# A two-layer diffusion backbone: the gating layer's mixing as plain fp32 matmuls, and another issue order

## The chip, the cores and the metric

The kernel runs on one core of a Trainium2 chip. Everything is fp32 in and fp32 out. The metric is the device time of one launch in microseconds; the time of a kernel is the median of several executions. The engines of the core are TensorE (PE, with its weight loads listed as PEld), VectorE (DVE), ScalarE (ACT), GpSimd (POOL) and SyncE (SP, which here only issues DMAs). Each engine works off its own queue in order; engines wait for each other by semaphores.

## The reference

512 latent tokens and 256 context tokens of width 1024 go through two layers. Only the latent tokens of the end are returned.

```python
for i in range(2):
    h = modulate(rmsnorm(x, g0), shift, scale)            # shift, scale, gate: rows of silu(c) @ ada_w[i] + ada_b[i]
    y = window_sink_mixer(h, h_ctx, ...) if i == 0 else chunk_gmlp(h, ...)
    x = x + gate * rmsnorm(y, g1)
    f = swiglu(modulate(rmsnorm(x, g2), shift_f, scale_f), w_in, w_out)     # hidden width 2816
    x = x + gate_f * rmsnorm(f, g3)

def chunk_gmlp(h, w_in, b_in, ln_g, ln_b, w_s, b_s, w_o):
    u, v = split(gelu(h @ w_in + b_in))                   # 512 x 1024 each
    v = layernorm(v, ln_g, ln_b)                          # as 4 chunks of 128 tokens, 8 groups of 128 columns
    mixed = einsum('gpq,bnqgc->bnpgc', w_s, v) + b_s      # per group and chunk: 128x128 by 128x128
    return (u * mixed) @ w_o
```

Layer 0 is attention over windows of 128 tokens and all of the context, with 16 heads on 4 key/value heads and a sink logit for each head. Layer 1 is the gating layer, `chunk_gmlp`, whose mixing the change is about.

## The kernel before, in words

**Precision by splits.** A matmul of the type fp32r takes fp32 operands that have been rounded to fewer bits. Nearly every product in the kernel is made of three of them: each operand is split into a high part (a cast on ACT, `high`, line 217) and the rest (a subtraction on DVE, `low`, line 220), and PE adds high by high, high by low and low by high into one PSUM bank (`mm3`, lines 269 to 271; `mm_a`, line 277). The weights come from HBM in units of 1 MB (`wfetch_N` on the SP queue) into one of two raw buffers, are split in halves (`whigh_N_h` on ACT, `wlow_N_h` on DVE) and are used from the split buffers. The in-projection of the feed-forward network (line 1445) and its out-projection (lines 1623 and 1650) combine blocks of operands first, so that fewer products are needed.

**The order of the work.** The string `ORDER` at line 41 is a list of step names written out by hand. A function hands a step to `at()`, with a rough time; `run_plan()` issues the steps of each stage in the order of the string. As each engine's queue is in order, the string sets what each engine does when, the DMAs of SP and POOL among it. The last projection of a layer (`down`) lies outside of it and is put in order by the framework. A name that comes again in a later stage has `#2` or `#3` behind it.

**The front.** Tiles of x are fetched (`x_fetch_t`, 4 and 5 are the context), normalised (`norm_in_t_z`, line 477 on DVE), turned by PE (`turn_in`, line 500) and modulated; `kv_k_t` are the key and value products of row block k and tile t, `ada0_rows` the first modulation rows.

**The seam between attention and its feed-forward network.** For each of four token tiles t, `ctshift_x_z` makes the modulated input in two halves (DVE, line 1166), `ctturn_z` turns it on PE into a PSUM bank (line 1173), `ctturned_hi` and `ctturned_lo` split it, and `f0head_h_s` are the first in-projection matmuls.

**The gating layer** (lines 1796 to 1947). `v_part` and `u_part` are the two halves of the in-projection; `u_part(u, z)` (lines 1867 to 1874) is 24 matmuls of 512 columns into a PSUM bank. Each of the four `VChain`s (line 1826) takes 128 tokens of v: `add`, `gelu`, `mean`, `var`, `rstd`, `gain` (layer norm times its gain, in place) and `bias` (line 1856, in place); `hi` and `lo` then split the result into `v_hi` and `v_lo`. `ws_in` fetches the mixing weights (512 KB) into one of the two raw buffers of the weight stream, `ws_high` and `ws_low` split them into `ws_hi` and `ws_lo`. `mixed(g)` (line 1883) makes, for group g, four products of 128x128 by 128x128 in one bank, each by `mm3`. `mixed_bias(g)` and `mixed_u(g)` (DVE) add the bias and multiply by gelu(u). The output projection y follows (line 277, weight units 51 to 54).

**The modulation rows** of this layer (`m2`, `m4`) are worked out meanwhile: `fetch_chunk` (SP, 512 KB each, eight of them), `add_chunk` (DVE, line 379), `fold` (a POOL DMA that adds the upper 64 partitions to the lower, line 393), `mirror` (an SP DMA back), `stack` (an ACT cast and a DVE subtraction of 64 partitions), `total` (a matmul with ones into a PSUM bank, line 406) and `done` (DVE or ACT reads the bank, lines 417 and 419).

**PSUM.** The matmul banks come from one pool of eight slots, given out in turn: a step that needs a slot waits until the readers of the bank that had it are done.

Of the kernel before, what the change touches and what calls it, by code (L numbers as in the profile page):

```python
# [14 lines left out]
P = 128  # L15
D = 1024
# [25 lines left out]
x_fetch_4 square_in_4 x_fetch_1 square_in_1 warm_0 rstd_in_4 warm_1 dma rstd_in_1 x_fetch_5 square_in_5 warm_2 warm_3  # L42
rstd_in_5 wfetch_0_0 norm_in_5_1 x_fetch_2 norm_in_4_0 dma#2 norm_in_1_0 turn_in_4_0 square_in_2 norm_in_1_1 warm_4
x_fetch_0 x_fetch_3 square_in_0 norm_in_5_0 turn_in_1_0 rstd_in_2 turn_in_1_1 norm_in_2_0 turn_in_5_0 ada0_fetch_0
turned_in_4_0 square_in_3 rstd_in_0 turned_in_5_0 turned_in_1_0 turn_in_5_1 ada0_rows_0 turn_in_2_0 rstd_in_3
norm_in_2_1 ada0_rows_out_0 norm_in_3_1 <lambda> norm_in_0_0 norm_in_3_0 ada0_cols_0 turn_in_3_1 turned_in_5_1
ada0_fetch_1 turn_in_0_0 norm_in_0_1 ada0_done_0 turn_in_2_1 ada0_fetch_2 whigh_0_0 wfetch_0_1 ada0_rows_1
modulate0_ctx_0 turn_in_0_1 turn_in_3_0 turned_in_3_1 modulated_ctx_0 ada0_rows_out_1 ada0_fetch_3 turned_in_1_1
wlow_0_0 turned_in_2_0 ada0_fetch_4 ada0_cols_1 turned_in_0_0 turned_in_3_0 ada0_rows_2 modulate0_0 wfetch_1 dma#5
# [2013 lines left out]
```

## Time and profile before

| | before |
|---|---|
| time, median of 3 runs | 1115.71 us (1113.52 to 1122.0) |
| the profiled execution: its time | 1122.28 us |
| its span | 1120.5 us |
| its mean granted TensorE clock | 0.993 |
| busy: PE, PEld | 98%, 86% of the span |
| busy: DVE, ACT, POOL | 85%, 55%, 22% |
| HBM | 171.71 MB read, 155 GB/s |

The page of the profile is one execution. Starts in its timelines are microseconds from the start of the span. An engine's row has the start, the duration, the line of the kernel, the operation, output and inputs, the tile sizes, and in brackets the idle time before it with what ended it. Matmuls overlap each other: the time that one costs PE is the distance from its start to the next one's, not its duration. "PEclk" is the clock that TensorE was granted, in tenths of full speed, in 40 slices of 28 us.

### The profile page before, as it was taken

To read this page: it belongs to the slowest core of one execution; us is meant where nothing else is said; L and a number is where in the kernel's file an instruction comes from. 1 tells how busy PE (TensorE), PEld (TensorE's weight loads), DVE (VectorE), ACT (ScalarE), POOL (GpSimd) and SP (SyncE) were. 2 spreads that over 40 slices of the span, in tenths; PEclk is the share of its full clock that TensorE was granted. 3 is DMA by queue.
4 is the path that set the end of the run, shared out by engine and by line. 5 is a ranking of instruction groups with operands and counts; after the bars stand their busy time and mean duration, and the time that the engine had idled before them with its cause. 6 is when DMAs were issued, how large, how long until landed. Compare 5 with 4: busy or idle time off the path is not lost.

```text
span 1120.5 us, 17907 instructions
## 1 busy us (share of the span) xinstructions
PE 1095.7 (98%) x7004; PEld 964.8 (86%) x7004; DVE 957.2 (85%) x1422; ACT 618.5 (55%) x1064; POOL 247.9 (22%) x239
## 2 busy tenths in 40 slices
PE   7999999999999999999999999999999999999997
PEld 4688887777899999997888787888899999998886
DVE  5888989958999999978987778777988898878985
ACT  6357677756555555545655544337555455556652
POOL 1416575624500000001322310005500000002400
PEclk9999999999999999999999999799999999999999
DMA  9642433243345655459954286653134333369821
GB/s 366 255 145 97 162 94 113 76 142 103 114 148 174 206 184 175 161 176 335 223 83 151 101 293 215 180 169 106 47 132 152 132 125 125 147 208 314 174 37 75
DMA packets 49017, 179.69 MB, mean 160 GB/s; under 512 B 4890, under 2 KB 9242, under 8 KB 37796
## 3 DMA queue, kind: packets, MB, share of 16 engines
q1 hardware_dynamic: 41300, 163.60, 42.0%
q0 software_dynamic: 7632, 14.95, 7.7%
q8 instruction: 55, 0.90, 0.3%
q14 instruction: 30, 0.25, 0.1%
HBM read 171.71 MB, written 2.10 MB: 155 GB/s over the span
## 4 chain that ended last, share of the span: by engine, by line
PE 84%; DVE 7%; DMA 3%; ACT 2%; issue 2%; POOL 1%; SPq 0%; DVEq 0%; POOLq 0%; ACTq 0%
PE f L1445 33%; PE y L1623 13%; PE y L277 4%; PE y L1650 4%; PE v L277 4%; PE s_ps L901 3%; PE o_ps L954 3%; PE pT_ps L934 3%; PE q_ps L269 1%; PE q_ps L271 1%; PE q_ps L270 1%; DMA acc<-acc 1%; DVE w_lo L220 1%; PE fa L271 1%; PE fa L269 1%
## 5 line engine op out<-in xcount | busy, mean ns | idle before, releaser
L1445 PE MATMUL f<-H,w_hi 128*128 128x256 f32 x960 | 178.4, 284 | 0.2 <-DVE fc L1456 0.2
L1445 PEld LDWEIGHTS f<-H,w_hi 128*128 128x128 f32 x960 | 149.9, 192 | 1.1 <-DVE fc L1456 0.7
L1445 PE MATMUL f<-H,w_lo 128*128 128x256 f32 x480 | 135.8, 283 | 0.0
L1623 PE MATMUL y<-w_hi,s 128*128 128x512 f32 x448 | 120.1, 389 | 0.0
L1445 PE MATMUL f<-S,w_hi 128*128 128x256 f32 x640 | 118.6, 283 | 0.0
L217 ACT CAST w_hi<-w_raw 128x1024 fp32r<-128x1024 f32 x90 | 94.5, 1052 | 37.7 <-PE v L277 9.7
L217 ACT CAST w_hi<-T 128x1024 fp32r<-128x1024 f32 x80 | 83.6, 1047 | 54.2 <-PE f L1445 32.1
L220 DVE TENSOR_TENSOR w_lo<-w_raw,w_hi 128x1024 fp32r<-128x1024 f32 (+1 forms) x81 | 95.1, 1180 | 8.7 <-ACT w_hi L217 8.7
L1452 ACT COPY fc<-f 128x256 f32<-128x256 f32 x120 | 44.7, 373 | 102.4 <-PE f L1445 99.5
L1445 PEld LDWEIGHTS f<-S,w_hi 128*128 128x128 f32 x640 | 100.0, 192 | 0.1
L1623 PEld LDWEIGHTS y<-w_hi,s 128*128 128x128 f32 x448 | 84.1, 188 | 17.5
L220 DVE TENSOR_TENSOR w_lo<-T,w_hi 128x1024 fp32r<-128x1024 f32 x80 | 97.3, 1216 | 0.0
L1445 PEld LDWEIGHTS f<-H,w_lo 128*128 128x128 f32 x480 | 92.1, 192 | 0.0
L393 POOL DMA_DIRECT2D acc<-acc x9 | 7.8, 862 | 377.2 <-DVE acc L379 371.7
L1445 PE MATMUL f<-S,w_lo 128*128 128x256 f32 x320 | 90.6, 283 | 0.5 <-DVE w_lo L220 0.5
L379 DVE SCALAR_TENSOR_TENSOR acc<-ada_k,sc,acc 128x1024 f32<-128x1024 f32 x56 | 71.6, 1278 | 11.9 <-DMA ada_k<-in_ada 9.8
L1611 POOL DMA_DIRECT2D t<-in_w x48 | 42.3, 938 | 125.3 <-issue 43.2
L1623 PE MATMUL y<-w_lo,s 128*128 128x512 f32 x224 | 69.1, 390 | 0.6 <-DVE w_lo L220 0.6
L1445 PE MATMUL f<-H,x 128*128 128x256 f32 x480 | 64.3, 283 | 0.0
L928 POOL TENSOR_SCALAR p<-p,st 128x512 f32<-128x512 f32 (+1 forms) x64 | 53.3, 850 | 45.6 <-DVE st L924 15.5
L277 PE MATMUL y<-w_hi,st 128*128 128x512 f32 x224 | 62.1, 391 | 0.0
L1445 PEld LDWEIGHTS f<-S,w_lo 128*128 128x128 f32 x320 | 61.4, 192 | 0.7 <-DVE w_lo L220 0.7
(263 smaller groups left out, 2909.7 us busy)
## 6 DMA issues: line engine op xcount, KB each, us to landing
w_raw<-in_w SPq DMA_DIRECT2D x67, 1024.0 KB, 5.1
ada_k<-in_ada SPq DMA_DIRECT2D x56, 512.0 KB, 5.4
ada_raw<-in_ada SPq DMA_DIRECT2D x12, 1024.0 KB, 4.9
w<-in_w SPq DMA_DIRECT2D x12, 1024.0 KB, 9.6
t<-in_w POOLq DMA_DIRECT2D x48, 256.0 KB, 5.7
ada<-in_ada SPq DMA_DIRECT2D x8, 1024.0 KB, 8.0
t<-in_w SPq DMA_DIRECT2D x8, 1024.0 KB, 9.4
w_raw<-in_w SPq DMA_DIRECT2D x10, 512.0 KB, 4.7
```

Of the source, the lines that this page charges most:

```text
L217: nc.scalar.copy(out=hi, in_=src)
L220: (eng or nc.vector).tensor_tensor(out=lo, in0=src, in1=hi.bitcast(F32), op=ALU.subtract)
L277: nc.tensor.matmul(dst, l, w[:, n * 512:(n + 1) * 512], start=first and i == 0, stop=last and i == 2)
L379: nc.vector.scalar_tensor_tensor(out=self.acc, in0=self.raws.pop(k), scalar=sc[:, k:k + 1], in1=self.acc, op0=ALU.mult, op1=ALU.add)
L901: nc.tensor.matmul(dst, self.qT[:, j, :], keys, start=i == 0, stop=i == 1)
L928: nc.gpsimd.tensor_scalar(out=p, in0=p, scalar1=self.st[:, 12 + j:13 + j], scalar2=1.0, op0=ALU.mult, op1=ALU.mult)
L934: nc.tensor.transpose(ps[:, j * P:(j + 1) * P], self.probs[j][:, i * P:(i + 1) * P], ident)
L1445: nc.tensor.matmul(dst, l[:, w], r[:, k, :], start=first and k == 0 and j == 0, stop=k == 3 and j == 2, skip_group_check=True)
L1452: nc.scalar.copy(out=self.c[n][:, i * 256:(i + 1) * 256], in_=self.ps[n, 1 if i == 1 else 0])
L1611: nc.gpsimd.dma_start(out=self.tt[:, p * D + 512 * i:p * D + 512 * (i + 1)], in_=a["w"][F2[self.layer] + 1 + 2 * p + i][:, c:c + 512], acc ...
L1623: nc.tensor.matmul(self.bank7(i, j), st[:, c:c + P], w[:, z * 512:(z + 1) * 512], start=i == 1 and p == 0 and l == 0 and z == 0, stop=p == ...
L1650: nc.tensor.matmul(self.y[t][n], st[:, x + t * P:x + (t + 1) * P], parts[h][w][:, n * 512:(n + 1) * 512], start=v == 0 and h == 0 and i == ...
```

## The change

*Mixing.* The mixing weights are fetched straight into an fp32 tile of their own, `ws`; `ws_high` and `ws_low` go. `VChain.bias` writes its result into one fp32 tile `v`; `hi` and `lo` go for all four tiles. `mixed(g)` calls `nc.tensor.matmul` once for each product, with fp32 operands.

*Order.* In front, the fetches of the two context tiles change places, `kv_0_4` comes earlier, `ada0_fetch_6` and `ada0_rows_3` later; a few first query products and splits swap. In attention and between the layers, some neighbouring steps change places. At the first seam `c1turn_1` moves behind `f0head_0_0`. In the gating layer `ws_in` moves from ahead of m2's third add to just ahead of `u_part_0_1`, and `wfetch_49` comes ahead of `m2fetch_gain`; `m4fetch_0` and `m4start` come behind `m2mirror`; `v2add` comes ahead of `m2done_0`; `m2done_512` moves from there to behind `v3norm`; `wlow_50_0` and `mixed_6` come ahead of the first `mixed_bias`; `whigh_51_0` comes behind `m4stack`, and `u_part_3_1` ahead of `wlow_51_0`.

```diff
@@ ORDER, front
-x_fetch_4 square_in_4 x_fetch_1 square_in_1 warm_0 rstd_in_4 warm_1 dma rstd_in_1 x_fetch_5 square_in_5 warm_2 warm_3
-rstd_in_5 wfetch_0_0 norm_in_5_1 x_fetch_2 norm_in_4_0 dma#2 norm_in_1_0 turn_in_4_0 square_in_2 norm_in_1_1 warm_4
+x_fetch_5 x_fetch_4 square_in_4 x_fetch_1 square_in_1 warm_0 rstd_in_4 warm_1 dma dma#2 square_in_5 warm_2 warm_3
+rstd_in_5 wfetch_0_0 rstd_in_1 x_fetch_2 norm_in_4_0 norm_in_5_1 norm_in_1_0 turn_in_4_0 square_in_2 norm_in_1_1
...
-wlow_0_0 turned_in_2_0 ada0_fetch_4 ada0_cols_1 turned_in_0_0 turned_in_3_0 ada0_rows_2 modulate0_0 wfetch_1 dma#5
-modulated_high_0 turned_in_2_1 ada0_rows_out_2 modulated_low_0 ada0_cols_2 kv_0_2 dma#4 kv_0_3 ada0_done_1
-ada0_fetch_6 kv_0_4 ada0_rows_3 modulated_high_1 modulate0_ctx_1 kv_0_5 ada0_done_2 modulate0_1 modulated_ctx_1
-whigh_0_1 modulated_low_1 norm_in_4_1 turn_in_4_1 m2start ada0_rows_out_3 turned_in_4_1 modulate0_ctx_2 kv_1_2 kv_1_4
...
+wfetch_1 dma#5 kv_0_4 modulated_high_0 turned_in_2_1 ada0_rows_out_2 modulated_low_0 ada0_cols_2 kv_0_2 dma#4 kv_0_3
+ada0_done_1 modulated_high_1 modulate0_ctx_1 kv_0_5 ada0_done_2 modulate0_1 modulated_ctx_1 whigh_0_1 modulated_low_1
+ada0_fetch_6 ada0_rows_3 norm_in_4_1 turn_in_4_1 m2start ada0_rows_out_3 turned_in_4_1 modulate0_ctx_2 kv_1_2 kv_1_4
...
@@ ORDER, first seam
-c2square_x c1turn_0 c3merge c2rstd_x c1turned_hi_0 c1turn_1 c1turned_lo_0 f0first_half_1 f0head_0_0 wfetch_12
+c2square_x c1turn_0 c3merge c2rstd_x c1turned_hi_0 c1turned_lo_0 f0first_half_1 f0head_0_0 c1turn_1 wfetch_12
...
@@ ORDER, gating layer
-wlow_47_0 m2add_chunk_1 v_part_3_(2,) v_part_1_(2,) v0add m2add_chunk_2 v0gelu m2fetch_chunk_5 wlow_47_1 v0mean ws_in
+wlow_47_0 m2add_chunk_1 v_part_3_(2,) v_part_1_(2,) v0add m2add_chunk_2 v0gelu m2fetch_chunk_5 wlow_47_1 v0mean
...
-m2fetch_gain#2 v_part_3_(3,) wlow_48_0 m4fetch_chunk_0 m4start#2 v1var v_part_2_(3,) ws_high m2mirror#2 v1rstd
-wfetch_49 v1gain v0hi ws_low v1norm m2stack#2 m4fetch_chunk_1 v1bias v0lo u_part_0_1 m2total_0_slot m2total_512_slot
-m2done_0#2 m2done_512#2 v2add m4add_chunk_0 m4fetch_chunk_2 whigh_49_0 u_part_1_0 v2gelu v1hi v1lo u_part_1_1 v2mean
+wfetch_49 v1gain m2fetch_gain#2 v_part_3_(3,) wlow_48_0 v1var v_part_2_(3,) m2mirror#2 m4fetch_chunk_0 m4start#2
+v1rstd v1norm m4fetch_chunk_1 v1bias m2stack#2 ws_in u_part_0_1 m2total_0_slot m2total_512_slot v2add m2done_0#2
+m4add_chunk_0 m4fetch_chunk_2 whigh_49_0 u_part_1_0 v2gelu u_part_1_1 v2mean v3add v2var wfetch_50 whigh_49_1
...
-gelu_u_1_1 v2hi v3bias v2lo m4add_chunk_6 v3hi v3lo m4add_chunk_7 m4fold#2 m4fetch_gain#2 mixed_0 whigh_50_1
-mixed_bias_0 mixed_1 mixed_u_0 mixed_bias_1 wlow_50_0 mixed_6 m4mirror#2 mixed_5 mixed_3 mixed_u_1 mixed_4
-mixed_bias_3 gelu_u_2_0 mixed_2 wlow_50_1 whigh_51_0 mixed_u_3 m4stack#2 u_part_3_0 whigh_51_1 mixed_bias_2 mixed_u_2
-wlow_51_0 m4total_0_slot mixed_bias_4 mixed_u_4 mixed_bias_5 gelu_u_2_1 wlow_51_1 mixed_u_5 u_part_3_1 mixed_bias_6
+v3bias m4add_chunk_6 m4add_chunk_7 m4fold#2 m4fetch_gain#2 mixed_0 wlow_50_0 mixed_6 m4mirror#2 whigh_50_1
+mixed_bias_0 mixed_1 mixed_u_0 mixed_bias_1 mixed_5 mixed_3 mixed_u_1 mixed_4 mixed_bias_3 gelu_u_2_0 mixed_2
+wlow_50_1 mixed_u_3 m4stack#2 whigh_51_0 u_part_3_0 whigh_51_1 mixed_bias_2 mixed_u_2 m4total_0_slot mixed_bias_4
+u_part_3_1 wlow_51_0 mixed_u_4 mixed_bias_5 gelu_u_2_1 wlow_51_1 mixed_u_5 mixed_bias_6 m4total_512_slot m4done_0#2
...
@@ gating layer
-    wsh = gp.tile([P, D], F32R, name="ws_hi")
-    wsl = gp.tile([P, D], F32R, name="ws_lo")
-    vhi = gp.tile([P, NT, D], F32R, name="v_hi")
-    vlo = gp.tile([P, NT, D], F32R, name="v_lo")
+    wsp = gp.tile([P, D], F32, name="ws")
+    vn = gp.tile([P, NT, D], F32, name="v")
...
     def ws_in():
-        got["ws"] = raw("ws_raw")[:, 0:D]
-        dma(got["ws"], a["ws"])
-
-    def ws_high():
-        high(wsh, got["ws"])
-
-    def ws_low():
-        low(wsl, wsh, got["ws"])
+        dma(wsp, a["ws"])
...
         def bias(self):
-            nc.vector.scalar_tensor_tensor(out=self.v, in0=self.v, scalar=self.r, in1=rows[2],
+            nc.vector.scalar_tensor_tensor(out=vn[:, self.t, :], in0=self.v, scalar=self.r, in1=rows[2],
                                            op0=ALU.mult, op1=ALU.add)
-
-        def hi(self):
-            high(vhi[:, self.t, :], self.v)
-
-        def lo(self):
-            low(vlo[:, self.t, :], vhi[:, self.t, :], self.v)
...
         for n in range(NT):
-            mm3(ps[:, n * P:(n + 1) * P], vhi[:, n, c], vlo[:, n, c], wsh[:, c], wsl[:, c], True, True)
+            nc.tensor.matmul(ps[:, n * P:(n + 1) * P], vn[:, n, c], wsp[:, c], start=True, stop=True)
```

More of the change, by code (lines that the diff above doesn't have):

```diff
@@ L172 @@
 m2add_chunk_3 v0var v_part_1_(3,) v0gain whigh_48_0 m2add_chunk_4 m2fetch_chunk_6 v0norm m2add_chunk_5 m2fetch_chunk_7
-v_part_2_(2,) v0rstd whigh_48_1 v1add m2add_chunk_6 u_part_0_0 v1gelu m2add_chunk_7 v0bias v1mean m2fold#2 wlow_48_1
-m2fetch_gain#2 v_part_3_(3,) wlow_48_0 m4fetch_chunk_0 m4start#2 v1var v_part_2_(3,) ws_high m2mirror#2 v1rstd
-wfetch_49 v1gain v0hi ws_low v1norm m2stack#2 m4fetch_chunk_1 v1bias v0lo u_part_0_1 m2total_0_slot m2total_512_slot
-m2done_0#2 m2done_512#2 v2add m4add_chunk_0 m4fetch_chunk_2 whigh_49_0 u_part_1_0 v2gelu v1hi v1lo u_part_1_1 v2mean
@@ L197 @@
-f1diff_2_4 c3turned_lo_1#3 f1part_high_2_3 f1head_2_2 f1sum_high_S4 f1part_low_2_1 f1head_3_0 f1sum_low_S4
-f1part_low_2_2 f1head_3_1 f1sum_high_S3 wfetch_58 f1sum_high_S1 f1head_3_2 f1sum_low_S1 f1sum_low_S2 f1part_low_2_3
-f1sum_low_S3
+v_part_2_(2,) v0rstd whigh_48_1 m2add_chunk_6 v1add u_part_0_0 v1gelu m2add_chunk_7 v0bias v1mean m2fold#2 wlow_48_1
+wfetch_49 v1gain m2fetch_gain#2 v_part_3_(3,) wlow_48_0 v1var v_part_2_(3,) m2mirror#2 m4fetch_chunk_0 m4start#2
+v1rstd v1norm m4fetch_chunk_1 v1bias m2stack#2 ws_in u_part_0_1 m2total_0_slot m2total_512_slot v2add m2done_0#2
@@ new lines @@
+m4add_chunk_0 m4fetch_chunk_2 whigh_49_0 u_part_1_0 v2gelu u_part_1_1 v2mean v3add v2var wfetch_50 whigh_49_1
+gelu_u_0_0 v3gelu gelu_u_0_1 v2gain m4add_chunk_1 m4fetch_chunk_3 m4fetch_chunk_4 wlow_49_1 v2rstd m4add_chunk_2
+v3mean wlow_49_0 u_part_2_0 v2norm v3var v2bias m4fetch_chunk_5 wfetch_51 v3rstd m4add_chunk_3 m4add_chunk_4
+m4fetch_chunk_6 u_part_2_1 v3norm m2done_512#2 whigh_50_0 v3gain m4add_chunk_5 m4fetch_chunk_7 gelu_u_1_0 gelu_u_1_1
+v3bias m4add_chunk_6 m4add_chunk_7 m4fold#2 m4fetch_gain#2 mixed_0 wlow_50_0 mixed_6 m4mirror#2 whigh_50_1
@@ new lines @@
+mixed_bias_0 mixed_1 mixed_u_0 mixed_bias_1 mixed_5 mixed_3 mixed_u_1 mixed_4 mixed_bias_3 gelu_u_2_0 mixed_2
+wlow_50_1 mixed_u_3 m4stack#2 whigh_51_0 u_part_3_0 whigh_51_1 mixed_bias_2 mixed_u_2 m4total_0_slot mixed_bias_4
+u_part_3_1 wlow_51_0 mixed_u_4 mixed_bias_5 gelu_u_2_1 wlow_51_1 mixed_u_5 mixed_bias_6 m4total_512_slot m4done_0#2
+m4done_512#2 gelu_u_3_0 gelu_u_3_1 mixed_7 mixed_u_6 mixed_bias_7 mixed_u_7 whigh_55_0 work_2_0#2 work_3_0#2
+whigh_55_1 c0square_y#3 work_2_1#2 work_3_1#2 wfetch_56 whigh_56_0 wlow_55_0 whigh_56_1 work_2_2#2 c1square_y#3
@@ L200 @@
+f1sum_a_S2#2 f1sum_a_S4 f1sum_a_S1#2 f1head_1_2 f1head_2_0 f1head_2_1 f1sum_a_S4#2 f1sum_high_S2 f1diff_2_4
+c3turned_lo_1#3 f1part_high_2_3 f1head_2_2 f1sum_high_S4 f1part_low_2_1 f1head_3_0 f1sum_low_S4 f1part_low_2_2
+f1head_3_1 f1sum_high_S3 wfetch_58 f1sum_high_S1 f1head_3_2 f1sum_low_S1 f1sum_low_S2 f1part_low_2_3 f1sum_low_S3
 """.split()
@@ L1908, in backbone_kernel @@
         at(3 + 2 * h, ws.low, GU, h, nc.vector)
-    at(0, ws_high)
-    at(1, ws_low)
     at(1.9, lend_u0)
```

163 lines of the change are left out of this document (77 added, 86 removed).

## The prediction

> **What bounds the kernel now.** I read the page first: busy time by engine, the slices with the granted clock, the chain that ended last.
>
> ```profile
> span 1120.5 us, 17907 instructions
> PE 1095.7 (98%) x7004; PEld 964.8 (86%) x7004; DVE 957.2 (85%) x1422; ACT 618.5 (55%) x1064; POOL 247.9 (22%) x239
> PEclk9999999999999999999999999799999999999999
> PE 84%; DVE 7%; DMA 3%; ACT 2%; issue 2%; POOL 1%; SPq 0%; DVEq 0%; POOLq 0%; ACTq 0%
> ```
>
> TensorE (PE) carries 84% of the chain and is busy nearly throughout, so an edit is worth what it takes from PE's own stream or from the few places where PE waits. VectorE (DVE), at 85%, is the engine that can take over. One slice stands out: the clock is full everywhere but in slice 26, which is where the gating layer mixes. So next came the windows and PE's timeline there.
>
> ```profile
> 700.00:705.70 5.70, 4.89 (x37) 4.48 (x36) 5.23 (x6) 3.18 (x4) 1.42 (x2) 1.00 0.41 166
> 705.70:710.00 4.30, 4.30 (x23) 4.30 (x22) 2.87 (x4) 0.00 (x0) 0.37 (x1) 0.51 0.80 178
> ...
> 720.00:725.00 5.00, 5.00 (x23) 4.10 (x22) 4.33 (x6) 0.88 (x2) 0.00 (x0) 1.00 0.46 169
> ```
>
> After the stretch come PE, PEld, DVE, ACT and POOL busy, the granted clock (1.00, 0.51, 1.00), the DMA share and GB/s.
>
> ```profile
> 701.53 0.22 PE L269 MATMUL mix<-ws_hi,v_hi 128*128 128x128 f32 x1
> ...
> 701.70 0.27 PE L271 MATMUL mix<-ws_hi,v_lo 128*128 128x128 f32 x1
> ...
> 702.59 0.27 PE L270 MATMUL mix<-ws_lo,v_hi 128*128 128x128 f32 x1
> 703.68 0.33 PE L271 MATMUL mix<-ws_hi,v_lo 128*128 128x128 f32 x1 [0.81 <-DVE v_lo L220]
> ...
> 713.76 0.41 PE L270 MATMUL mix<-ws_lo,v_hi 128*128 128x128 f32 x1
> 713.97 0.41 PE L271 MATMUL mix<-ws_hi,v_lo 128*128 128x128 f32 x1
> ...
> 717.38 0.73 PE L1872 MATMUL u<-H,w_hi 128*128 128x512 f32 x1
> ...
> 720.27 0.39 PE L1874 MATMUL u<-H,w_lo 128*128 128x512 f32 x1
> ...
> 731.12 0.69 PE L277 MATMUL y<-w_hi,st 128*128 128x512 f32 x2
> ```
>
> The step from start to start is what a matmul costs PE: 0.11 us in mixing at full clock, 0.21 from 705.7 on.
>
> **The mixing, which is the change's core.** Before, it is 32 products of 128x128 by 128x128, each as three matmuls (lines 269 to 271).
>
> ```profile
> L271 PE MATMUL mix<-ws_hi,v_lo x32: 273/415/415, 701.7 to 731.0; 128*128 128x128 f32 x32
> L220 DVE TENSOR_TENSOR v_lo<-vtmp,v_hi x4: 1217/1218/1225, 675.0 to 702.4; 128x1024 fp32r<-128x1024 f32 x4
> ```
>
> At full clock that is 96 x 0.11 = 10.6 us. After, it is 32 plain fp32 products. This kernel has plain fp32 matmuls at full size only at its start, on the idle tile, 512 columns wide: each is two records, and at full clock a record starts 0.43 us after the last.
>
> ```profile
> 6.59 0.19 PEld L485 LDWEIGHTS warm<-idle 128*128 128x128 f32 x1 [0.24 <-issue]
> 7.02 0.19 PEld L485 LDWEIGHTS xT<-idle 128*128 128x128 f32 x1 [0.24 <-issue]
> ```
>
> The split matmuls of 512 columns step by 0.23 (679.97 to 680.20 below), so a plain record streams its columns twice. A plain record of 128 columns should then cost what a split matmul of 256 columns costs. Three of those (L1445) take 0.36 us:
>
> ```profile
> 306.54 0.40 PE L1445 MATMUL f<-S,w_hi 128*128 128x256 f32 x2
> 306.78 0.28 PE L1445 MATMUL f<-S,w_lo 128*128 128x256 f32 x1
> 306.90 0.40 PE L1445 MATMUL f<-S,w_hi 128*128 128x256 f32 x2
> ```
>
> That is 0.12 each, with the weight load hidden. So 32 x 2 x 0.12 = 7.7 us, against 10.6: **-2.9 us**. The bounds are a quarter of the wide record, 0.43/4 = 0.107 (6.9 us), and load and stream one after the other, 0.11 + 0.12 = 0.23 (14.7 us, a loss of 4.1). I take 0.12, the row of the same streaming length.
>
> **The clock.** From 705.74 to 717.38 mixing runs at half clock: the seven groups before that point (84 matmuls) take 717.38 - 701.53 = 15.85 us, less the wait of 0.98 (703.68 - 702.59, less its own 0.11), so 14.87 in place of 9.3. The first eight matmuls of u_part_3 then take 720.27 - 717.38 = 2.89 us in place of 1.81. Together **-6.6 us** if the clock stays up. Why it fell, I can only read from where it did: PE streams 128 columns per 0.11 us there, about half the time, and had just waited a microsecond. The L1445 stage streams 256 per 0.12, and no slice of it is below full clock. The new records look like that stage, so I forecast no fall. [...]
>
> **Two waits go.** In front of u_part_1_0, PE waits for a row sum to be read (its slot is freed by m2done_0, line 419); the new order puts v2add ahead of m2done_0, which frees another slot sooner. In mixing, PE waits for the last v_lo, which no longer exists.
>
> ```profile
> 678.45 0.63 PE L406 MATMUL ada_ps<-acc_st,ones 128*128 128x512 f32 x2
> 679.63 0.50 PE L1872 MATMUL u<-H,w_hi 128*128 128x512 f32 x1 [0.55 <-DVE row L419]
> 679.97 0.39 PE L1873 MATMUL u<-H,w_hi 128*128 128x512 f32 x1
> 680.20 0.39 PE L1874 MATMUL u<-H,w_lo 128*128 128x512 f32 x1
> ```
>
> The first is 679.63 - 678.45 less two matmuls of 0.23, and about 0.1 us of slower start behind it: 0.8. The second is 0.98. **-1.8 us**. PE's stream from 678.45 to the first y matmul at 731.12, 52.7 us, thus shrinks by 2.9 + 6.6 + 1.8 = 11.3; y could start at 719.8.
>
> **What is late next.** DVE loses four v_lo (4.9 us), one low part of the weights and nothing else; ACT loses the five casts. DVE's remaining work has to follow PE forward. The chain that decides is the last modulation row (m4): DVE's last add, the fold by POOL's DMA, the mirror by SP, ACT's cast, DVE's low half, then PE's m4total_0 in the middle of u_part_3.
>
> ```profile
> 698.35 1.27 DVE L1856 SCALAR_TENSOR_TENSOR vtmp<-vtmp,rv,row 128x1024 f32<-128x1024 f32 x1
> ...
> 703.54 1.28 DVE L379 SCALAR_TENSOR_TENSOR acc<-ada_k,sc,acc 128x1024 f32<-128x1024 f32 x1
> ...
> 715.21 1.22 DVE L220 TENSOR_TENSOR acc_st<-acc,acc_st 64x1024 fp32r<-64x1024 f32 x1 [0.28 <-ACT acc_st L217]
> ```
>
> ```profile
> 704.70:731.10 26.40, 26.40 (x128) 24.14 (x128) 21.23 (x26) 7.33 (x10) 0.84 (x1) 0.74 0.64 180
> ```
>
> From the end of the last add (704.8) to the end of the low half (716.4) are 11.6 us of DMA and casts that nothing shortens. PE will reach m4total_0 at 700.7 (mixing starts 0.8 sooner) + 28 x 0.24 + 24 x 0.227 = 712.9. If the last add moves only by the v_lo ahead of it, the sum is there at 715.2 and PE waits 2.3 us. If it moves by all four v_lo and by the order that lets v2add run in DVE's idle time before m2done_0, it comes some 4 us sooner and PE waits nothing. whigh_51_0, now behind m4stack on ACT, and mixed_bias_2, wlow_51_0 and wlow_51_1 behind it on DVE, wait with it; the first y matmul needs them. Between 0 and 2.3, and up to 5 with the queue behind it (first rival), I take **+1.0**.
>
> Moves that cost nothing: ws_in goes to a tile of its own and later on SP, behind m4fetch_1; its 512 KB are wanted only by mixing, over 20 us on. The raw buffer it held goes back to the weight stream, so wfetch_49 need not wait for ws_low. m2done_512, moved behind v3norm, holds one PSUM slot longer; the slot is wanted by the fourth mixing group, so the cover is the whole of u_part_2 (10.9 us). m4fetch_0 and m4start go behind m2mirror on SP; the first add comes over 8 us later.
>
> **The seam at 275 us.** c1turn_1 moves behind f0head_0_0, into PE's wait of 1.26 us. But the next transposes wait for the same engine:
>
> ```profile
> 277.12 0.63 PE L1173 MATMUL hT<-ident,tmp 128*128 128x128 f32 x4 [1.26 <-DVE tmp L1166]
> ...
> 283.07 1.03 PE L1173 MATMUL hT<-ident,tmp 128*128 128x128 f32 x8
> ```
>
> ```profile
> 281.68 1.41 DVE L1166 SCALAR_TENSOR_TENSOR tmp<-tmp,rx,row 128x512 f32<-128x512 f32 x2
> ```
>
> DVE makes c2's two halves until 283.1, and PE transposes them at 283.07. A PE that is early waits there: **-0.3**, between 0 and -1.3.
>
> **The front.** The order of the fetches changes (context rows 5 before 4), but PE's last wait there ends with norm_in_4_1 on DVE, which comes behind the same DVE steps as before:
>
> ```profile
> 31.02 0.63 PE L500 MATMUL xT<-ident,xin 128*128 128x128 f32 x4 [1.72 <-DVE xin L477]
> ```
>
> kv_0_4 and ada0_rows_3 only change places with other PE work ahead of that wait. 0, between -0.6 and +0.6. The swaps in attention and the other seams reorder work that PE does without waiting: 0, within 1 either way.
>
> **The sum.** -2.9 - 6.6 - 1.8 + 1.0 - 0.3 = -10.6 on the span of 1120.5, so 1109.9; the profiled execution took 1122.28, 1.8 more than its span, hence **1111.7 us**. The median before is 1115.71, which is 6.6 under the profiled execution: just what the half clock cost it. I read the median as a run whose clock did not fall, and 1122.0 among the three as one whose clock did. Then the change is worth 4.0 us against the median, 0.4%, and the forecast stays 1111.7. About 1% is what a measurement of this kernel can tell from no change: faster is under 1104.6, slower over 1126.9.
>
> **The rivals and the chances.**
> - Forecast, 1109 to 1114: 0.55.
> - DVE becomes the bound in mixing. For it: 21.23 us of DVE work between 704.7 and 731.1, which from 703.5 would end at 724.7, 5 us behind PE's 719.8. Against it: some of that work (third-row adds, later groups) need not precede y. 1111.7 + 5 - 1 = 1115.7: 0.13.
> - The clock falls all the same. [...] A fall of the same length costs the 6.6 again: 1118.3: 0.09.
> - The gap of profiled to timed executions is the profiler's own, in every run. Then the timed kernel gains all of it: 1115.71 - 10.6 = 1105.1. Against it: 1122.0 among the timed runs. 0.13, half of it past 1%.
> - Slower: the plain product is four passes of 128 columns, each with its own load, half streaming as in the old mixing, and the clock falls as there. At 0.21 a pass, 32 x 4 x 0.213 = 27.3 us against the 16.2 that the old mixing took in this profile, so 1122.3 + 11.1 - 2.1 = 1131; it decides once a product costs over 0.5 us. Against it: two records, not four, on the idle tile. 0.04. [...]
> - The moves together gain more (all of the seam's 1.3, the front's 0.6, attention's 1, and the wait at m4total none, and 3 from DVE that no row shows): about 1104: 0.06.
>
> Range 1105 to 1117: all of the first, most of the second and fourth, a little of the others, 0.8. Faster by over 1%: 0.12; slower by over 1%: 0.04; the rest 0.84.
>
> **What the profile after would show.** 64 records of mix with steps of 0.12 us (0.11 to 0.23 the bounds); the slice of mixing at clock 9; no wait of u L1872 for row L419; the first y matmul some 20 us after the first mixing record, where it was 29.6 (731.12 - 701.53). Wrong would be: a clock under 1.00 in mixing, a wait of PE for acc_st or w_lo over 2 us, or a first kv stage that moves by over a microsecond.

## The result and the profile after

| | before | after |
|---|---|---|
| time, median | 1121.47 us (20 runs, 1113.52 to 1125.38) | 1113.17 us (20 runs, 1111.02 to 1115.41) |
| ratio after to before | | 0.9943, 95% interval 0.9925 to 0.9961 |
| profiled execution: time, span | 1122.28 us, 1120.5 us | 1113.02 us, 1111.3 us |

The change saves 0.6%: a real gain, under the 1% of the forecast's bounds. The forecast was 1111.7 us.

The median before has moved from 1115.71 to 1121.47 because the executions of the kernel before fall into two groups: those in which TensorE's clock fell in the gating layer, and those in which it didn't. Over all the runs of this study there are 57 of the first kind (1119.96 to 1125.38, median 1122.6) and 46 of the second (1113.29 to 1117.05, median 1115.4). The mean granted clock of an execution tells them apart where it was recorded: 0.989 to 0.993 for 45 of the first kind, 0.995 to 0.999 for 38 of the second. Where in the kernel the clock fell is seen in one profile only; its 13.65 us at half clock (705.82 to 719.47) cost 6.8 us, about the gap between the two medians. Of the three runs that the prediction had, two were of the second kind. The changed kernel has one group, 0.995 to 0.999. So the change is worth some 9 us in executions whose clock fell, and 2 us in the others.

First the page of the changed kernel, as it was read before: span, engines, the clock in 40 slices, the chain by engine.

```profile
span 1111.3 us, 17832 instructions
PE 1088.7 (98%) x6972; PEld 956.4 (86%) x6972; DVE 951.4 (86%) x1417; ACT 613.0 (55%) x1059; POOL 246.4 (22%) x239
PEclk9999999999999999999999999999999999999999
PE 84%; DVE 7%; DMA 3%; issue 2%; ACT 2%; POOL 1%; SPq 0%; DVEq 0%; POOLq 0%; ACTq 0%
```

The dip of the clock in the gating layer is gone; what bounds the kernel is the same. Next the groups of instructions on the tile `mix` (least, median and greatest duration, then first and last start), and PE's timeline there.

```profile
L1871 PE MATMUL mix<-ws,v x64: 270/275/275, 702.8 to 721.2; 128*128 128x128 f32 x64
```

```profile
702.82 6.41 PE L1871 MATMUL mix<-ws,v 128*128 128x128 f32 x56
708.99 0.48 PE L1856 MATMUL u<-H,w_hi 128*128 128x512 f32 x1
...
714.54 0.39 PE L405 MATMUL ada_ps<-acc_st,ones 128*128 128x512 f32 x1
...
720.45 1.05 PE L1871 MATMUL mix<-ws,v 128*128 128x128 f32 x8
721.26 0.71 PE L276 MATMUL y<-w_hi,st 128*128 128x512 f32 x2
```

32 products are 64 records. 56 of them take 708.99 - 702.82 = 6.17 us, 0.110 each. No row has a bracket: PE waits neither for v nor for the row sum at 714.54. From the first mixing record to the first y matmul it is 18.4 us where it was 29.6. That is 11.2 us, but the span shrank by 9.2, and mixing begins at 702.82 where it began at 701.53: 1.3 us were lost ahead of it. The windows of the front (after the stretch PE, PEld, DVE, ACT and POOL busy, then the clock, the DMA share and GB/s) and PE's timeline say where the largest loss lies.

```profile
28.50:32.50 4.00, 1.42 (x12) 1.22 (x9) 3.19 (x4) 1.08 (x2) 2.26 (x1) 1.00 0.84 301
32.50:35.90 3.40, 3.40 (x11) 2.66 (x10) 2.81 (x8) 2.30 (x3) 1.57 (x1) 0.50 1.00 421
```

```profile
27.54 1.07 PE L521 MATMUL rows<-ada,s 128*32 128x256 f32 x16
...
31.19 0.63 PE L499 MATMUL xT<-ident,xin 128*128 128x128 f32 x4 [2.58 <-DVE xin L476]
...
83.40 0.63 PE L754 MATMUL qT_ps<-ident,qs 128*128 128x128 f32 x4
...
113.64 0.50 PE L405 MATMUL ada_ps<-acc_st,ones 128*128 128x512 f32 x1 [0.53 <-ACT qT L755]
```

The wait ahead of the last context transposes ends where it ended (31.19, before 31.02), but it is now one piece of 2.58 us (before 1.72), and behind it the clock is half for 3.4 us. The first query transposes come at 83.40; in the kernel before they came here:

```profile
81.07 0.63 PE L755 MATMUL qT_ps<-ident,qs 128*128 128x128 f32 x4
```

At 113.64 there is a wait in attention that the kernel before does not have.

### The profile page after: what moved, and what is told of

It is laid out like the page before. It is cut to its first block, busy times and chain, and to the rows that moved or that the text cites. A ratio compares the mean times of both kernels' runs of the same rounds, so it can differ in the third digit from the quotient of the medians.

```text
span 1111.3 us, 17832 instructions
## 1 busy us (share of the span) xinstructions
PE 1088.7 (98%) x6972; PEld 956.4 (86%) x6972; DVE 951.4 (86%) x1417; ACT 613.0 (55%) x1059; POOL 246.4 (22%) x239
## 4 chain that ended last, share of the span: by engine, by line
PE 84%; DVE 7%; DMA 3%; issue 2%; ACT 2%; POOL 1%; SPq 0%; DVEq 0%; POOLq 0%; ACTq 0%
PE f L1444 33%; PE y L1622 12%; PE y L276 5%; PE v L276 4%; PE y L1649 3%; PE s_ps L900 3%; PE o_ps L953 3%; PE pT_ps L933 3%; DVE w_lo L219 1%; PE u L1856 1%; PE u L1858 1%; PE u L1857 1%; PE q_ps L268 1%; DMA acc<-acc 1%; PE q_ps L270 1%
```

## The experiments

| kernel | median, us | ratio to before, 95% interval |
|---|---|---|
| the changed kernel | 1113.17 | 0.9943 (0.9925 to 0.9961) |
| e1: three front steps back | 1112.03 | 0.9932 (0.9910 to 0.9954) |
| e2: plain mixing alone | 1116.57 | 0.9969 (0.9946 to 0.9992) |
| e3: split, no wait for the last v_lo | 1116.10 | 0.9976 (0.9952 to 1.0000) |
| e4: new order, split mixing | 1118.66 | 0.9989 (0.9967 to 1.0011) |
| e5: old order of front and attention | 1110.25 | 0.9921 (0.9891 to 0.9951) |
| e6: e5, a cast later | 1109.14 | 0.9913 (0.9882 to 0.9943) |
| e7: e5, seam as before | 1110.60 | 0.9922 (0.9894 to 0.9949) |
| e8: wait of 2.3 us planted in plain mixing | 1116.82 | 0.9984 (0.9958 to 1.0011) |
| e9: v2add behind m2done_0 | 1113.56 | 0.9951 (0.9924 to 0.9978) |
| e10: wait of 1.2 us planted in plain mixing | 1119.65 | 1.0010 (0.9984 to 1.0036) |
| e11: old order of attention alone | 1110.96 | 0.9940 (0.9914 to 0.9965) |
| e12: e5, two low parts on VectorE | 1108.57 | 0.9908 (0.9876 to 0.9940) |

The share of executions before with a fallen clock differs from set to set (22 of 35, 9 of 18, 14 of 30), so the ratios of different sets are not compared closely; the medians are. Those of the executions before whose clock stayed up agree: 1115.06, 1115.33 and 1115.12. Below, "undisturbed" means these.

**e1, three steps of the front back.** Base: the changed kernel.

```diff
-wfetch_1 dma#5 kv_0_4 modulated_high_0 turned_in_2_1 ada0_rows_out_2 modulated_low_0 ada0_cols_2 kv_0_2 dma#4 kv_0_3
-ada0_done_1 modulated_high_1 ... whigh_0_1 modulated_low_1 ada0_fetch_6 ada0_rows_3 norm_in_4_1
+wfetch_1 dma#5 modulated_high_0 turned_in_2_1 ada0_rows_out_2 modulated_low_0 ada0_cols_2 kv_0_2 dma#4 kv_0_3
+ada0_done_1 ada0_fetch_6 kv_0_4 ada0_rows_3 modulated_high_1 ... whigh_0_1 modulated_low_1 norm_in_4_1
```

> The changed kernel with three steps of the front (kv_0_4, ada0_fetch_6, ada0_rows_3) back at their old places; its fetch order stays. Theory A (clock in front): in the changed kernel PE idles 2.58 us in one piece ahead of the last context transposes, and the granted clock is half for 3.4 us from 32.5 us on; with 0.7 us of kv work back in the middle of that idle time the piece is under 1.8 us, the clock stays full from 30 to 40 us, the first query transpose (qT_ps) starts near 82 us instead of 84.1, and the time is about 2 us under the changed kernel's: 1111. Rival B (the fetch order delays the front): qT_ps stays at 84, time within 0.5 us of the changed kernel's 1113.2.

1112.03, 1.1 us under the changed kernel, half of what theory A said. In its profile PE's wait is 1.74 us and the clock is full from 30 to 40 us, but this execution had half clock from 10.7 to 17.6 us already (the changed kernel's from 12.04 to 15.45; e1's mean clock over the span is 0.996), and is a microsecond later by then (line 522 at 28.50, the changed kernel's line 521 at 27.54). So its qT_ps stands at 82.9 and settles nothing. The direction agrees with A; e5 and e11 add to it.

**e2, plain mixing alone.** The kernel before with the changed code of mixing and its old order.

```diff
 def mixed(g):
-    mm3(ps[:, n * P:(n + 1) * P], vhi[:, n, c], vlo[:, n, c], wsh[:, c], wsl[:, c], True, True)
+    nc.tensor.matmul(ps[:, n * P:(n + 1) * P], vn[:, n, c], wsp[:, c], start=True, stop=True)
```

> The kernel before, its order kept, with the plain mixing alone (the removed steps left out). Theory A (the mixing is the gain, whatever the order): 64 records of mix at 0.11 us, clock full in mixing, no wait for v_lo; against an undisturbed 1115.6 of the kernel before, 10.6 - 7.05 = 3.5 us less for the matmuls and 1.0 less for the wait: 1111, and no run above 1116. Rival B (the order of the gating layer is needed too, DVE or m4 become late): 1113 or more, with a wait of PE over 1 us for acc_st or w_lo between mixing and the first y matmul.

Rival B by the time. Mixing itself is as fast as in the changed kernel (56 records in 6.17 us), but PE then waits. The waits of PE from 674 to 730 us (line waited for, total, times, longest):

```profile
PE y L276 <- DVE m L1875: 2.6, 1, 2.6
PE ada_ps L405 <- DVE acc_st L219: 0.8, 1, 0.8
PE u L1856 <- DVE row L418: 0.5, 1, 0.5
PE u L1858 <- DVE w_lo L219: 0.3, 1, 0.3
```

The wait that rival B named, for acc_st, is 0.8 us. The longest comes later, in the midst of y, and is for a PSUM bank: y needs one whose reader, a `mixed_bias` (line 1875), VectorE has not come to. VectorE's queue is late there not by its work alone: between 705 and 726 us its adds (line 378) wait 1.64, 0.31, 1.24 and 0.70 us for their fetches, and what stands behind them waits too. And the windows around PE's wait:

```profile
724.70:728.10 3.40, 0.98 (x5) 0.48 (x3) 2.70 (x4) 0.00 (x0) 0.00 (x0) 1.00 0.64 187
728.10:731.50 3.40, 3.21 (x8) 2.53 (x9) 3.40 (x4) 0.00 (x0) 0.00 (x0) 0.50 0.69 212
```

Behind that wait of 2.6 us the clock is at half for 3.4 us again. With the old order, plain mixing gains nothing over the undisturbed kernel before (1116.57 against 1115.1), and the three executions with a mean clock of 0.999 (1114.0, 1115.3 and 1115.6) gain nothing either: VectorE's queue became the bound.

**e3, split mixing without the wait.** The kernel before; the low term of the fourth chunk is the third chunk's.

```diff
-    mm3(ps[:, n * P:(n + 1) * P], vhi[:, n, c], vlo[:, n, c], wsh[:, c], wsl[:, c], True, True)
+    mm3(ps[:, n * P:(n + 1) * P], vhi[:, n, c], vlo[:, min(n, 2), c], wsh[:, c], wsl[:, c], True, True)
```

> The kernel before, but the fourth chunk of mixing takes the low part of the third chunk instead of its own, so that PE does not wait for the last v_lo (the low term of the fourth chunk is another chunk's; the amount of work is the same). Theory A (the wait made the clock fall): the clock stays full in mixing, the seven groups take 28 x 0.33 = 9.3 us, all runs near 1114.6. Rival B (the sparse stream, 128 columns in 0.11 us, is enough): no wait, but the clock is half for several us in mixing in the profile or in more than a third of the runs, times from 1114.6 to 1122.

Theory A for the clock: none of the 12 runs has a mean clock under 0.997, and all lie between 1113.65 and 1117.51. The windows over mixing, which runs from 699.89 to 709.2, and the row sum behind it:

```profile
700.00:705.00 5.00, 5.00 (x48) 5.00 (x46) 4.86 (x6) 1.55 (x3) 1.79 (x2) 1.00 0.28 81
705.00:709.00 4.00, 4.00 (x39) 4.00 (x37) 2.71 (x4) 0.00 (x0) 0.00 (x0) 1.00 0.71 172
```

```profile
715.87 0.47 PE L406 MATMUL ada_ps<-acc_st,ones 128*128 128x512 f32 x1 [0.94 <-DVE acc_st L220]
```

So the sparse stream alone (a matmul of 128 columns every 0.11 us) did not bring the clock down in these 12 runs; with the wait of 0.81 us in it, in the profile before, the clock fell. But the time is no better than the undisturbed kernel before (1116.1 against 1115.1, where 1114.6 was expected): the microsecond saved ahead is waited for at the row sum. What takes the rest is not settled; in this profile some y matmuls from 745 to 752 us step by 0.34 instead of 0.23, without a wait or a fall of the clock.

**e4, the new order with split mixing.** The changed kernel with `mm3`, casts and low parts put back (`v0hi` to `v3lo`, `ws_high`, `ws_low` near their old places).

```diff
-    nc.tensor.matmul(ps[:, n * P:(n + 1) * P], vn[:, n, c], wsp[:, c], start=True, stop=True)
+    mm3(ps[:, n * P:(n + 1) * P], vhi[:, n, c], vlo[:, n, c], wsh[:, c], wsl[:, c], True, True)
```

> The changed kernel's order with the split mixing put back (casts, low parts and the three matmuls of each product; the mixing weights through a raw buffer again). Theory A (the mixing carries the gain): undisturbed it is 3.5 us of matmuls and about 1 us of waiting over the changed kernel, 1117.7, and with the clock at half in mixing some 7 us more, 1125; so it is slower than the kernel before by the 2 to 3.5 us that the front and attention lose. Rival B (the order carries the gain): about 1113 to 1115, no fall of the clock.

1118.66 (1116.38 to 1121.86): 5.5 us over the changed kernel and 3.6 over the undisturbed one before. Its profiled execution (1116.41) is one of its fastest; there the seven groups take 9.32 us at full clock, and PE waits 1.25 us at 679.93 for a row sum's low half (m2's). VectorE is not what made it late:

```profile
678.65 1.22 DVE L220 TENSOR_TENSOR acc_st<-acc,acc_st 64x1024 fp32r<-64x1024 f32 x1 [5.26 <-ACT acc_st L217]
```

```profile
SPq L214 <- DVE w_lo L220: 14.8, 1, 14.8
```

It stood idle for 5.26 us until ACT's cast was done, ACT had waited for the mirror's DMA, and on the SP queue the mirror stood behind a weight fetch that waited 14.8 us for a raw buffer (until 669.38; the changed kernel issues that fetch at 659.31), since the mixing weights hold the other one again. Together with e2: neither the plain mixing in the old order nor the new order with split mixing is faster than the undisturbed kernel before. Of e4's 3.6 us, 2.9 are the front and attention (e5, next). With plain mixing, that is with VectorE's time and the raw buffer freed, the new order of the gating layer does gain: e5 takes 1110.25 where e2 takes 1116.57.

**e5, front and attention in the old order.** The changed kernel, with the old order string from its start to m3's third add, the last stretch of attention that differs.

```diff
-x_fetch_5 x_fetch_4 square_in_4 x_fetch_1 ... m3fetch_1 q_next_q_rows_6 ... value_6 q_step_7_5 q_step_7_6
+x_fetch_4 square_in_4 x_fetch_1 square_in_1 ... m3fetch_1 q_next_q_rows_6 ... value_6 q_step_7_5 q_step_7_6
```

> The changed kernel with the whole order of the front and the attention as before; from the first seam on it is the changed one. Theory A (front and attention of the new order cost what the profile says): in the profile of the changed kernel the second-layer work is 2.3 us late by the first query transpose and 3.5 us late at 186 us; with both back the time is 2 to 3 us under the changed kernel's 1113.2, so 1110 to 1111, and under the 1112.0 of the run with three steps of the front back. PE has no wait of 0.8 us for acc_st near 112 us. Rival B (the delays are the scatter of the front from run to run): within 0.7 us of 1113.2.

1110.25, 2.9 us under the changed kernel: theory A by the medians. The profile does not show it by the path expected: this execution's clock fell in the front as well, with the old order.

```profile
28.70:32.10 3.40, 1.67 (x16) 0.98 (x8) 2.79 (x2) 1.10 (x3) 2.41 (x1) 1.00 0.74 279
...
32.20:35.50 3.30, 3.30 (x10) 2.54 (x9) 3.00 (x6) 2.10 (x3) 0.67 (x1) 0.50 0.96 401
```

So that fall, 3.4 us at half clock, is no property of the new front alone. Of the profiles with the old front, two have it (e2 and e5, qT_ps at 83.3) and three don't (before, e3 and e7, 81.1 to 81.4); with the new front four have it (the changed kernel, e8, e9 and e10), and e4 and e11 don't (81.8). The fall costs 83.40 - 81.8 = 1.6 us. The new order by itself costs at most the rest, 0.4 to 0.8, since e4 and e11 also have half clock for 3.41 us near 12 us, and before, e3 and e7 don't (mean clocks of those profiles: 0.997 and 0.998 in e4 and e11, 0.999 in e3 and e7; before, the clock is full up to 705.82).

The falls begin elsewhere in each execution. In the changed kernel two of 3.41 us begin at 12.04 and 32.52 us, 20.48 us or six times 3.41 apart; in e10 they begin at 31.82 (below) and 717.90 us (further down):

```profile
28.41:31.82 3.41, 1.47 (x19) 0.46 (x17) 3.41 (x5) 2.23 (x4) 2.19 (x1) 1.00 1.01 397
31.82:35.23 3.41, 2.77 (x9) 2.41 (x10) 2.14 (x5) 0.60 (x2) 0.21 (x1) 0.50 0.92 376
```

What parts the executions no run shows. With the old front's wait of 1.72 to 1.74 us PE is busy 1.67 of the 3.40 us ahead of the fall in e2 and e5, and 1.68 of the 3.40 from 28.50 to 31.90 in the kernel before, where the clock stays full. With the new front's wait (2.58 us in the changed kernel) PE is busy 1.31 (the changed kernel), 1.47 (e10) and 1.50 us (e9) of the 3.4 ahead of the fall; from 28.50 to 32.50 it is busy 1.41 of 4.00 us in e11, which keeps full clock behind them, and 1.42 in the changed kernel, which doesn't. So whether the clock falls in the front is in part the luck of the execution.

**e6, a cast later.** Base: e5.

```diff
-modulated_ctx_1 whigh_0_1 modulated_low_1 norm_in_4_1 turn_in_4_1 m2start ada0_rows_out_3 turned_in_4_1
+modulated_ctx_1 modulated_low_1 norm_in_4_1 turn_in_4_1 m2start ada0_rows_out_3 whigh_0_1 turned_in_4_1
```

> As the run before it (old front and attention), and the cast of the second half of the first key/value unit (whigh_0_1) is issued later on ACT, behind the copy of a modulation row, so that POOL's subtraction of that half does not run beside VectorE's last normalisation of a context tile. Theory A (the two share something: that normalisation takes 2.6 us beside POOL, and the same shape is far shorter elsewhere): it takes under 1 us, PE's wait of 1.72 us ahead of the last context transposes is gone, the clock has one cause less to fall, 1.5 to 2 us less than the run before it: 1109. Rival B (other VectorE work is slowed by POOL instead, or the normalisation is slow by itself): within 0.7 us of the run before it.

Both in part. The normalisation takes 0.48 us instead of 2.59, and PE's wait ahead of the transposes is gone. But POOL's subtraction now lies beside the next VectorE operation of that kind:

```profile
30.43 2.40 POOL L219 TENSOR_TENSOR w_lo<-w_raw,w_hi 128x1024 fp32r<-128x1024 f32 x1 [13.05 <-ACT w_hi L216]
...
30.90 2.08 DVE L562 TENSOR_SCALAR hfc<-cnT,sb 128x256 f32<-128x256 f32 x1
```

It ends with POOL's (32.98 and 32.83), and PE waits 1.07 us behind it. Gain over e5: 1.1 us by medians of six runs each, whose ranges overlap.

**e7, the seam as before.** Base: e5.

```diff
-c2square_x c1turn_0 c3merge c2rstd_x c1turned_hi_0 c1turned_lo_0 f0first_half_1 f0head_0_0 c1turn_1 wfetch_12
+c2square_x c1turn_0 c3merge c2rstd_x c1turned_hi_0 c1turn_1 c1turned_lo_0 f0first_half_1 f0head_0_0 wfetch_12
```

> As the first run of this set (old front and attention), and c1turn_1 back ahead of the first in-projection matmuls, as it was. Theory A (the move closed the whole wait): PE waits 1.2 to 1.5 us again at the transposes near 276 us and the time is 1.3 us more than the first run's. Rival B, the term of the prediction (0.3 us, since the next transposes wait for VectorE anyway): at most 0.5 us more.

1110.60 against 1110.25: rival B, within what can be told. And its profile, like that of e3, has the old order and no wait:

```profile
275.57 0.60 PE L1172 MATMUL hT<-ident,tmp 128*128 128x128 f32 x4
```

The 1.26 us of the profile before were an accident of that execution, in which VectorE was 1.5 us later behind an equally early PE (its scaling of the second half began at 276.23, in e3 at 274.76, with the transposes of the token tile before at 268.90 and 268.94).

**e8 and e10, a wait planted in plain mixing.** The changed kernel; the last step of the fourth chunk is issued behind m4's adds, three times (e8) or twice (e10).

```diff
-v3bias m4add_chunk_6 m4add_chunk_7 m4fold#2
+m4add_chunk_6 m4add_chunk_7 v3bias m4fold#2
...
         def bias(self):
+          for _ in range(3 if self.t == 3 else 1):    # e10: 2
             nc.vector.scalar_tensor_tensor(out=vn[:, self.t, :], in0=self.v, scalar=self.r, in1=rows[2],
```

> The changed kernel, and the last step of the fourth chunk of v (its scaling and shift) is issued behind the last adds of m4 and three times over, so that plain mixing waits for it about 1 us, as split mixing waited for v_lo in the kernel before; the result is the same. Theory A (what counts is how much PE streams in some 3.4 us: plain records are as dense as 256-column matmuls): the wait is there, the clock stays full in mixing. Rival B (a wait of that length in mixing makes the clock fall by itself): the clock is half for 3.4 us or more behind it, in the profile or in a third of the runs, with 2 us or more of time. By both the time is 1 to 4 us over the changed kernel's 1113.2, for VectorE's 2.6 us more work.

> As the planted wait of 2.5 us, with the last step of the fourth chunk twice instead of three times, so that plain mixing waits about 1.3 us, near the 1.0 us of the kernel before. Theory A (streaming in some 3.4 us counts): of any 3.4 us over 1.9 are dense work, 55%, so the clock stays full in mixing, and the mean clocks of the runs are those of the changed kernel (0.995 to 0.999); time 1.3 to 2 us over 1113.2. Rival B (a wait of over 1 us in mixing is enough): half clock for 3.4 us behind it in the profile or in a third of the runs.

e8: the wait came out at 2.31 us, not 1, and the clock fell. Timeline and windows of e8:

```profile
705.43 6.80 PE L1872 MATMUL mix<-ws,v 128*128 128x128 f32 x44 [2.31 <-DVE v L1847]
```

```profile
703.00:706.50 3.50, 1.19 (x11) 1.07 (x10) 3.46 (x4) 0.00 (x0) 0.00 (x0) 1.00 0.79 201
706.50:709.90 3.40, 3.40 (x18) 3.40 (x18) 3.23 (x6) 0.00 (x0) 0.00 (x0) 0.50 0.46 100
709.90:713.00 3.10, 3.10 (x29) 3.06 (x29) 1.74 (x2) 2.66 (x3) 0.00 (x0) 1.00 0.39 151
```

It came back after 3.4 us, with mixing still running, where split mixing was at half for 13.65 us, past its seventh group. e10, with 1.24 us, is the like of the kernel before, and there the clock stayed up through mixing:

```profile
706.05 5.85 PE L1872 MATMUL mix<-ws,v 128*128 128x128 f32 x50 [1.24 <-DVE v L1847]
...
717.87 0.79 PE L1859 MATMUL u<-H,w_lo 128*128 128x512 f32 x1 [2.76 <-DVE w_lo L219]
```

```profile
704.20:707.60 3.40, 2.16 (x20) 1.97 (x18) 2.89 (x3) 0.00 (x0) 0.53 (x1) 1.00 0.89 213
...
714.50:717.90 3.40, 0.64 (x4) 0.22 (x2) 3.10 (x4) 3.40 (x6) 0.00 (x0) 1.00 0.19 72
717.90:721.30 3.40, 3.40 (x8) 2.72 (x9) 3.34 (x5) 0.60 (x2) 0.00 (x0) 0.50 0.87 282
```

So in this profile theory A holds for mixing. Its time was missed by 5 us: the edit pushed the low part of unit 50 back on VectorE, behind an add that waited 2.56 us for its DMA; PE waited 2.76 us for it, and then the clock fell. That later fall makes the clocks of e10's runs useless for the question, so it rests on the one profile.

**e9, v2add behind m2done_0.** Base: the changed kernel.

```diff
-m2total_512_slot v2add m2done_0#2 m4add_chunk_0
+m2total_512_slot m2done_0#2 v2add m4add_chunk_0
```

> The changed kernel with v2add back behind m2done_0, as before. Theory A (the term of the prediction): PE waits some 0.7 us for line 419's reader (here line 418) in front of u_part_1_0 again, and all of it stays: 0.8 us over the changed kernel's 1113.2. Rival B (PE is early there and waits later for something else, or the reader is early enough now that the low parts of v and of the mixing weights are gone from VectorE): within 0.3 us of 1113.2 and no wait over 0.5 us near 680 us.

The wait is back in the profile as before (0.55 us for line 418, 0.94 from start to start); the time, 1113.56, is 0.4 over the changed kernel's. The sign is that of theory A, the size between A and B and within the scatter.

**e11, attention alone in the old order.** Base: the changed kernel.

```diff
-q_step_3_10 exp_2_1 q_step_3_11 ... normalise_7_1 value_5 turn_7_0 total_8 ... score_9_3 block_10 turn_7_1
+q_step_3_10 q_step_3_11 ... normalise_7_1 value_5 turn_7_0 m3fetch_gain ... m3add_0 turn_7_1 q_next_q_split_5
```

> The changed kernel with the order of the attention as before, front as changed. Theory A (the profile): PE's waits of 0.8 us for acc_st near 112 us and 0.6 us near 147 us are gone, 1.2 us under the changed kernel's 1113.2: 1112.0, and the front accounts for the rest of the 2.9 us that front and attention cost together. Rival B (the front is all of it): within 0.4 us of 1113.2.

1110.96, 2.2 us under the changed kernel, and PE has no wait from 100 to 160 us. So attention's reordering costs most of the 2.9 us that front and attention cost together; 1.2 of it are seen in the profiles: from the row sum at 105.96 to the one at 164.32 the changed kernel takes 58.4 us where before, e5 and e11 take 56.5, and from there to the first seam's transposes it takes 0.7 us less than they do. The rest is not placed.

**e12, two low parts on VectorE.** Base: e5.

```diff
-            at(n - .8, ws.low, KV0 + u, h, nc.gpsimd)
+            at(n - .8, ws.low, KV0 + u, h, nc.vector if k < 2 else nc.gpsimd)
```

> Old order of front and attention, rest changed (as the run of 1110.3 us), and the low parts of two halves of the first key/value units are made by VectorE (1.2 us each) instead of POOL (2.4 us each). Theory A (a VectorE operation of the TENSOR_SCALAR kind stands still until POOL's subtraction ends, 2.1 to 2.6 us for 0.2 to 0.5 us of work): the normalisation takes 0.5 us, PE's wait ahead of the last context transposes falls under 0.5 us, no VectorE operation there takes over 2 us, and the time is 1.5 to 2.5 us under 1110.3: 1108.3. Rival B (VectorE is full there, so its 2.4 us of new work costs as much as the standing still): 1109.5 to 1110.5.

Theory A: 1108.57 (1106.24 to 1110.77), 1.7 us under e5, 4.6 under the changed kernel and under the undisturbed kernel before in every run. The front of e12 on VectorE:

```profile
28.54 0.48 DVE L476 TENSOR_SCALAR xin<-xin,r 128x512 f32<-128x512 f32 x1
...
30.64 0.41 DVE L562 TENSOR_SCALAR hfc<-cnT,sb 128x256 f32<-128x256 f32 x1
```

One operation behind them (line 540, at 35.4) still takes 2.16 us. The first query transposes come at 79.5 us, and the clock does not fall there. e12 beats both kernels.

## Why the prediction was right or wrong

The time lies in the range, 1.5 us over the forecast, and the case named likeliest is the one that came. That it came so near is in part luck. Laid side by side, the two profiles differ by +2.3 us up to the first query transposes, +1.2 from there to the first seam, -1.4 in the seam, -0.8 from there to mixing, -11.2 from mixing to y and +0.7 behind it, -9.2 in all. The forecast had 0, 0, -0.3, -0.8, -9.5 and 0: misses of 4.2 us one way and 2.8 the other. Step by step:

- **The mixing (-2.9).** Right, a little small: two records a product, each near a 256-column matmul in cost, at 0.110 us instead of 0.12, so 64 x 0.110 = 7.0 and -3.5. The lower bound, a quarter of the wide plain record, was the better row. The slower rival's four passes with a load each no run shows: the 32 products are 64 records with 64 loads.
- **The clock (-6.6).** Right, and so was the reading of the three timed runs: 46 of 103 executions before have no fall. The text gave two reasons, half the time streaming and a wait of a microsecond, and did not choose; in e3 and e10 neither alone was enough. Without the wait the sparse stream kept the clock (e3, 12 runs with mean clocks of 0.997 or more); with a dense stream a wait of 1.24 us did not cost it (e10, one profile). The rival by which the clock falls in mixing all the same did not come: it is 1.00 from 702.80 to 721.30. Why split mixing went with a fall in 57 executions and with none in 46 is not shown: no profile of those 46 was kept.
- **Two waits (-1.8).** Both are gone, but a wait that is gone is not time saved: e3 takes one away and is no faster, as PE waits at the row sum instead. e9 puts the other back for 0.4 us rather than 0.8, within the scatter.
- **What is late next (+1.0).** Nothing: PE meets the row sum at 714.54 without waiting. The sum would have been 1.0 better for it. But the text mis-sized what makes it so: "moves that cost nothing" treats the gating layer's order as neutral, and e2 shows that it is what keeps VectorE's queue ahead; e4 shows that without the raw buffer which the move gives back, a row sum comes 1.25 us late. With the old order the forecast's first rival comes true, 1116.57 against its 1115.7.
- **The seam (-0.3).** The term held (e7: 0.35, no more than the scatter), although the 1.26 us of the profile before are all gone in the profile after: that wait was an accident of one execution.
- **The front (0, up to +0.6).** The order itself costs at most 0.4 to 0.8 us, about the bound. But the first kv stage moved by 2.3 us, which the prediction had named as a sign of being wrong. What failed is that the step looked only at when PE's wait ends, not at whether the clock falls behind it: half clock behind the piece of 2.58 us is 1.6 us more in this profile, and e2 and e5 show that the old front's 1.72 us can cost it too.
- **Attention (0, within 1).** Wrong in size: 2.2 us by e11's median, 1.2 by the profiles. "Reorder work that PE does without waiting" looked only at the waits of before, and the new wait for the reader of a bank (113.64, 0.53 us) is one that the order made.

## What to carry to other kernels

When a change takes work off an engine, look at that engine's queue as closely as at the one that gains: here the cheaper mixing gained nothing until the order of VectorE and the fetches was changed to use the time (e2 against e5). A wait of PE was priced here not by its length alone but by what PE streamed around it: 0.81 us in split mixing went with 13.65 us at half clock, 1.24 us in plain mixing (e10) with none. And the price differed from execution to execution: the old front's wait of 1.72 to 1.74 us went with 3.4 us at half clock in e2 and e5 and with none in the kernel before and in e7. So make the stream around an unavoidable wait dense, or split the wait (e1: 1.74 us in place of 2.58, and full clock from 30 to 40 us). And before a single profile's wait goes into a sum, ask for a second execution: the seam's 1.26 us and the front's fall were each there in one and not in another.

## What the runs showed of the hardware

The clock was at half for 3.41 us (the changed kernel, 12.04 to 15.45 and 32.52 to 35.94) or for 13.65 (the kernel before, 705.82 to 719.47). Of the falls profiled behind a wait of PE, the shortest wait was 0.81 us (before, in mixing) and the longest 2.76 (e10). The old front's wait of 1.72 to 1.74 us went with a fall in e2 and e5 and with none in the kernel before, e3 and e7. In the falls profiled behind a wait PE was busy 0.64 to 1.67 us in the 3.4 us ahead (0.64 in e10's later one, 0.98 in e2's later one, 1.31 in the changed front, 1.67 in e5's front; in e8 1.19 of 3.50); e10's mixing, busy 2.16 us of 3.4 with dense records, kept it. Busy time alone doesn't part them: PE was busy 1.41 of the 4.00 us from 28.50 to 32.50 in e11, which kept the clock, and 1.42 in the changed kernel, which lost it. In the kernel before, PE was busy 2.59 us of the 3.4 ahead of the fall, but by an estimate from the steps (128 columns at the rate of a 512-column matmul, 0.227 / 4 = 0.057 us, in every 0.11) it streamed half of that, 1.3 us. By the same estimate e3's stream is 1.8 us in 3.4 and kept the clock, while behind the fall the clock was still at half at 717.38, where the stream of the kernel before (0.11 of every 0.21 us) ended. What comes between 1.3 and 1.8 no run shows.

A VectorE operation of the TENSOR_SCALAR kind that met a subtraction on POOL in these traces took 2.59 us instead of 0.48 (line 477 before, line 476 in e12) or 2.08 instead of 0.41 (line 562 in e6, in e12). It ended just behind POOL's, by 0.28 us in the kernel before and 0.15 in e6.

```profile
28.16 2.43 POOL L220 TENSOR_TENSOR w_lo<-w_raw,w_hi 128x1024 fp32r<-128x1024 f32 x1 [11.31 <-ACT w_hi L217]
28.28 2.59 DVE L477 TENSOR_SCALAR xin<-xin,r 128x512 f32<-128x512 f32 x1
```

What makes them late beside POOL no run shows.
